# Layer 1 of an S5 and attention encoder: fourteen gate tiles as block quads ahead of k, q and v, branch b inside the S5 stage

## The chip, the cores and the metric

The kernel runs on one core of one Trainium2 chip. The time is the device time of that core in microseconds (us); the time before is the median of three runs. Engines are named as in the profile: PE (TensorE, matrix products), DVE (VectorE), ACT (ScalarE), POOL (GpSimd, here mainly an issuer of DMAs) and SP (SyncE, the issuer of most loads).

## The reference

Two layers, each a token mixer and a feed-forward network, on x of 1024 tokens by 1024 channels, in float32. Of one layer:

```python
hn = rmsnorm(h, norm1_g[layer])
proj = hn @ w_in[layer]          # u 512, q 512, k 128, v 128, gate_a 1024, gate_b 1024
gate_a = sigmoid(proj[..., o_ga:o_gb]); gate_b = sigmoid(proj[..., o_gb:])
y_a = s5_branch(u, ...)          # bidirectional diagonal state space, gelu, GLU
y_b = windowed_gqa(q, k, v, sink, bias, mask)   # 8 heads, window 128
merged = gate_a * (y_a @ w_branch_a[layer]) + gate_b * (y_b @ w_branch_b[layer])
h = h + merged @ w_out[layer]
hn2 = rmsnorm(h, norm2_g[layer])
h = h + (silu(hn2 @ ffn_w_gate[layer]) * (hn2 @ ffn_w_up[layer])) @ ffn_w_down[layer]
```

## The kernel before

Activations lie channels on partitions, in two halves of 512 tokens. A float32 product is three products of fp32r pairs (a high part and a rest): weight high by activation high, weight high by activation low, weight low by activation high. `chain` (L166) does that for each of the K blocks of 128, so a half tile of the input projection (K = 1024, tile `pj`) is 24 matmuls of 128x512, and a half tile of a branch product (K = 512, tile `br`) is 12. `piece` (L179) is the same for one block product of a quad. `fetch` (L116) loads a weight tile with a DMA on SP's queue into one of four buffers `raw`; `parts` (L154) splits it, ACT casting the high part `whi` (L163), DVE subtracting the low part `wlo` (L164).

A quad replaces two tiles over both halves, a 2x2 product of blocks that would take eight block products of 12 matmuls, by seven products of sums of blocks, after Strassen and Winograd. The FFN uses it for gate and up tiles (`quad_items`, L1235): `quad_part` (L130) forms and splits the sums of the weights, `sums` (L1215) those of the activations (`T`, four lists of pairs).

The work is a list of items (`self.seq`) that `build` (L1353) writes in order and `emit` (L193) carries out; weights are split ahead of their use by a few items. Each engine runs its instructions in the order written, with small shifts by the scheduler.

In layer 1, before the change, the order is: the k, v and q tiles, woven with the norm of the second half (`norm_parts`, L1134); the first half tiles of u; `attention_items` (L849), 18 steps. In a step PE does scores `s` of one block, the value product `pv` of an earlier one and the transposes `pt`; DVE does the exponentials' sums and scales (L780, L797). One fill item, a projection half tile of q, u or a gate, is added per step (`per` = 1). From step 12 each step also has one S5 state: `s5_states` (L913), in which PE does 16 small products (`s5x`, L924), DVE the rotation, the scans and the rotation back (L932 to L948), and ACT four copies (`s5sg`, L952). Then `s5_items` (L1007): in each of eight iterations two states, one output (`s5y` on PE, L966 to L969, from the copies of two states), one gelu (DVE L981, ACT tanh L982, DVE L989), the loads of two later states on SP (L899 to L909), and two fill items, the gate tiles that are left. A gate tile (`tile_gate`, L746) ends with a tanh on ACT (L751) and a store to DRAM on POOL's queue (L753). `att_pairs` (L829) splits the attention's output of one group of heads into pairs (ACT L841, DVE L842); in layer 1 both groups come behind the S5 stage, with the GLU (`glu_items`, L1069). Last come the items of branch b and of branch a in turns (`branch_items`, L1046).

Layer 0 has the other order already: its gate tiles are fills of attention and S5, the first pairs stand at step 11 of attention, and its branch-b items fill the S5 stage at 2.2 per iteration together with the gates that are left.

Of the kernel before, what the change touches and what calls it, by code (L numbers as in the profile page):

```python
# [17 lines left out]
P = 128  # L18
# [3 lines left out]
HC = 512  # L22
# [73 lines left out]
class Trunk:  # L96
# [752 lines left out]
    def attention_items(self, l, keys, q23, fill, per, tail):  # L849


        stage = {}
        fill = (list(fill[:2]) if l else []) + q23 + list(fill[2 if l else 0:])

        def scores(u):
            stage[u] = self.att_scores(l, u // 8, u % 8)

        def scale(u):
            self.att_scale(l, u // 8, *stage[u])

# [240 lines left out]
        return early, split, out  # L1101


    def w_out_items(self, l):
        nc, V = self.nc, self.nc.vector
        self.h2 = {}
# [2 lines left out]
        src = self.t["xt"] if l == 0 else self.hs  # L1109
# [43 lines left out]
    def ffn_items(self, l, fill, head):  # L1153

        nc, V = self.nc, self.nc.vector
        ff = [{}, {}]
        quads = QUAD_FROM[l]
        groups = GROUPS[l]
        last = len(groups) - 1
        early = quads < 4  # L1160
        ys = {} if early else None
# [48 lines left out]
        n0, n1 = (self.norm_parts(h, "rf", 2 * l + 1, lambda m, h=h: self.h2[m, h], lambda: self.hn2, ys) for h in range(2))  # L1210
        main = []
        blocks = []
        T = [[None] * 4 for _ in range(4)]

        def sums(j):  # L1215

            at = ((j, 0), (j, 1), (j + 4, 0), (j + 4, 1))
            if early:
                y11, y12, y21, y22 = (ys.pop(a) for a in at)
            else:  # L1220
                y11, y12, y21, y22 = (self.A("y") for _ in at)
                for y, (m, h) in zip((y11, y12, y21, y22), at):
                    hi, lo = self.hn2[h][m]
                    V.tensor_tensor(y, hi.bitcast(F32), lo.bitcast(F32), ADD)
            V.tensor_tensor(y11, y12, y11, SUB)
            V.tensor_tensor(y12, y22, y12, SUB)
            V.tensor_tensor(y22, y22, y11, SUB)
            V.tensor_tensor(y21, y21, y22, SUB)
            for k, y in enumerate((y11, y22, y12, y21)):
                T[k][j] = (y, None)  # L1230

        def sum_pairs(j, k):
            T[k][j] = self.split(T[k][j][0], f"tt{k}")

        def quad_items(f):  # L1235

            q = Quad(self.t["w_gate"][l, f].rearrange("p k c -> p (k c)"), self.t["w_up"][l, f].rearrange("p k c -> p (k c)"))
            b = {}

            def product(bank, g, off, xs, start):  # L1240
                def run():
                    if start:
                        b[bank] = self.PS(f"q{bank}")
                    self.piece(b[bank], g, off, xs(), start)
                return (run, g)

            B = lambda h, a: lambda: self.hn2[h][a:a + 4]
            p = [product("x", q.a, 0, B(0, 0), True), product("y", q.b, HC, lambda: T[1], True),
                 product("v", q.b, 0, lambda: T[0], True), product("x", q.a, HC, B(0, 4), False),
                 product("y", q.c, 0, lambda: T[2], False), product("w", q.d, 0, lambda: T[3], True),  # L1250
                 product("v", q.e, 0, B(1, 4), False)]

            def first():
                b["p1"] = self.A("qp")
# [91 lines left out]
        if fill:  # L1346
            a = len(head) + 12
            b = fill_end
# [4 lines left out]
    def build(self):  # L1353
# [31 lines left out]
        for l in range(DEPTH):  # L1385
# [23 lines left out]
            n0, n1 = (self.norm_parts(h, "ra", 2 * l, lambda m, h=h, src=src: src(m, h), lambda: self.hn) for h in range(2))  # L1409
            v1, v2 = self.halves(vc[0])  # L1410
            loads, states = self.s5_head(l)
            tail_items = {11: pairs[:1] if l == 0 else []}
            for k, (ld, sts) in enumerate(zip(loads, states)):
                a = 18 - 2 * S5_LEAD + k
                tail_items.setdefault(a - 2, []).append(ld)
# [21 lines left out]
            else:  # L1437

                k1, k2 = self.halves(kc[0])
                self.add(tail[:-6] + [n0[0]] + tail[-6:-4] + [n0[1], n0[2], tail[-4], n0[3], tail[-3], n0[4], tail[-2], n0[5],  # L1440
                                                              tail[-1], (start_layer,)] +
                         [k1, n1[0], k2, v1, n1[1], n1[2], v2, n1[3], n1[4], n1[5], qc[0], ke[0], ve[0], qe[0], kc[1], ke[1],
                          vc[1], ve[1]] + keys[:2] + [qc[1], qe[1], vals, bias0] + q1 + us[:2])
# [23 lines left out]
            self.add(early[:3] + split[:3] + left[:n // 2] + early[3:] + (pairs[:1] if l else []) + left[n // 2:n] + split[3:] +  # L1467
                     (self.mix(glu, pairs[1:]) if l else glu))
            left = left[n:]
            if l == 0:  # L1470
                rest = left + ba
            else:
# [141 lines left out]
```

## Time and profile before

| what | us |
|---|---|
| median of three runs | 2656.34 (2655.23 to 2657.16) |
| the profiled execution, its own time | 2654.39 |
| its span on the core | 2652.6 |
| PE busy | 2595.7 |
| DVE busy | 1646.7 |
| ACT busy | 1027.1 |

The span is the stretch from the first to the last instruction; 1.8 us of the execution's time lie around it. The granted clock of PE was 0.993 of full speed on average. A matmul's row lasts 0.39 us from its start to its modelled end, but the next one starts before that: rates are read from starts.

### The profile page before, as it was taken

The numbers are of one execution on the slowest core, as the hardware profiler recorded it, in microseconds if no ns is written. First come the engines' busy times: TensorE is split into PE (matmuls) and PEld (weight loads), VectorE is DVE, ScalarE is ACT, GpSimd is POOL, SyncE is SP. The second block draws the span as 40 slices with busy tenths as digits, with TensorE's granted clock in tenths as the row PEclk, the third lists the DMA queues.
The fourth block names the chain that finished last, engine by engine and source line by source line (L and its number), as shares of the span: only waits on it lengthen the run. The fifth ranks groups of instructions, "written<-read, shape, count | busy, mean of one in ns | idle before, by whom it ended". The sixth has DMA issues, their size and how long they took to land.

```text
span 2652.6 us, 35154 instructions
## 1 busy us (share of the span) xinstructions
PE 2595.7 (98%) x12914; PEld 2112.6 (80%) x12914; DVE 1646.7 (62%) x3481; ACT 1027.1 (39%) x1953; POOL 346.3 (13%) x508
## 2 busy tenths in 40 slices
PE   8999999999999999999999999999999999999997
PEld 6786677887888888888877778888878888888886
DVE  8985878565955655544673576646376545554556
ACT  5335653422333233333344553343235433333332
POOL 0231001000122110121010001100002221122010
PEclk9999999999999999999999999999999999999998
DMA  3453345353255252564342235434315652465253
GB/s 138 144 177 114 125 135 180 123 190 136 70 123 149 89 106 51 120 126 89 78 178 76 72 128 181 149 119 168 127 64 114 132 123 62 91 122 114 60 109 132
DMA packets 153981, 317.16 MB, mean 120 GB/s; under 512 B 20384, under 2 KB 53408, under 8 KB 153808
## 3 DMA queue, kind: packets, MB, share of 16 engines
q1 hardware_dynamic: 105040, 201.68, 23.4%
q0 software_dynamic: 48768, 113.24, 19.5%
q8 instruction: 101, 1.65, 0.2%
q14 instruction: 72, 0.59, 0.1%
HBM read 196.37 MB, written 118.44 MB: 119 GB/s over the span
## 4 chain that ended last, share of the span: by engine, by line
PE 90%; DVE 6%; DMA 2%; ACT 1%; issue 1%; SPq 0%; DVEq 0%; ACTq 0%
PE pj L175 6%; PE pj L176 6%; PE pj L177 6%; PE dn L175 6%; PE dn L176 6%; PE dn L177 6%; PE br L175 2%; PE br L177 2%; PE br L176 2%; PE wo L175 2%; PE wo L176 2%; PE wo L177 2%; PE qy L187 2%; PE qx L187 2%; PE qx L186 2%; PE qy L186 2%
## 5 line engine op out<-in xcount | busy, mean ns | idle before, releaser
L164 DVE TENSOR_TENSOR wlo<-raw,whi 128x1024 fp32r<-128x1024 f32 (+3 forms) x208 | 192.6, 926 | 291.3 <-ACT whi L163 284.4
L163 ACT CAST whi<-raw 128x1024 fp32r<-128x1024 f32 (+3 forms) x208 | 168.6, 811 | 400.3 <-PE pj L176 120.5
L175 PE MATMUL pj<-rah,whi 128*128 128x512 f32 x768 | 306.7, 400 | 0.7 <-ACT rah L112 0.7
L176 PE MATMUL pj<-ral,whi 128*128 128x512 f32 x768 | 301.1, 392 | 1.3 <-DVE ral L113 1.3
L177 PE MATMUL pj<-rah,wlo 128*128 128x512 f32 x768 | 300.2, 391 | 0.0
L1192 POOL DMA_DIRECT2D hs<-dx x192 | 165.3, 862 | 818.7 <-ACT dx L1191 708.3
L175 PEld LDWEIGHTS pj<-rah,whi 128*128 128x128 f32 x768 | 144.9, 189 | 35.0 <-issue 3.1
L176 PEld LDWEIGHTS pj<-ral,whi 128*128 128x128 f32 x768 | 145.2, 189 | 31.2 <-DVE ral L113 3.0
L177 PEld LDWEIGHTS pj<-rah,wlo 128*128 128x128 f32 x768 | 144.9, 189 | 30.9
L1191 ACT COPY dx<-dn 128x512 f32<-128x512 f32 x192 | 111.7, 583 | 86.8 <-PE dn L177 80.9
L780 DVE CUSTOM_DVE_ANT_0 x<-s,bias,nsink 128x384 f32<-128x384 f32 (+1 forms) x128 | 67.8, 580 | 67.4 <-PE s L774 65.8
L952 ACT COPY s5sg<-s5s 64x256 f32<-64x256 f32 x128 | 51.7, 404 | 133.8 <-DVE s5s L947 126.1
L175 PE MATMUL wo<-mgh,whi 128*128 128x512 f32 x256 | 100.0, 391 | 0.0
L177 PE MATMUL wo<-mgh,wlo 128*128 128x512 f32 x256 | 99.7, 389 | 0.0
L176 PE MATMUL wo<-mgl,whi 128*128 128x512 f32 x256 | 99.6, 389 | 0.0
L186 PE MATMUL qx<-rfh,whi 128*128 128x512 f32 x256 | 99.6, 389 | 0.0
L187 PE MATMUL qx<-rfl,whi 128*128 128x512 f32 x256 | 99.6, 389 | 0.0
L188 PE MATMUL qx<-rfh,wlo 128*128 128x512 f32 x256 | 99.6, 389 | 0.0
L112 ACT CAST ffah<-ts 128x512 fp32r<-128x512 f32 x32 | 19.9, 621 | 174.3 <-DVE ts L1274 174.3
L784 ACT ACTIVATE x<-x,sm 128x384 f32<-128x384 f32 (+1 forms) x128 | 73.9, 578 | 21.0 <-DVE sm L780 17.5
L175 PE MATMUL dn<-ffbh,whi 128*128 128x512 f32 x208 | 81.9, 394 | 0.0
L176 PE MATMUL dn<-ffbl,whi 128*128 128x512 f32 x208 | 81.2, 390 | 0.0
(435 smaller groups left out, 6748.6 us busy)
## 6 DMA issues: line engine op xcount, KB each, us to landing
hs<-dx POOLq DMA_DIRECT2D x192, 256.0 KB, 5.7
raw<-in_w_in SPq DMA_DIRECT2D x52, 512.0 KB
raw<-in_w_gate SPq DMA_DIRECT2D x44, 512.0 KB
raw<-in_w_up SPq DMA_DIRECT2D x44, 512.0 KB
g<-th POOLq DMA_DIRECT2D x64, 256.0 KB, 2.8
thr<-g SPq DMA_DIRECT2D x64, 256.0 KB
raw<-in_w_down SPq DMA_DIRECT2D x80, 192.0 KB
hs<-h POOLq DMA_DIRECT2D x48, 256.0 KB, 2.3
```

The costliest lines, as they stand in the source:

```text
L163: nc.scalar.copy(g.hi[:, :n], g.raw[:, :n])
L164: nc.vector.tensor_tensor(g.lo[:, :n], g.raw[:, :n], g.hi[:, :n].bitcast(F32), SUB)
L175: mm(ps, lhsT=wh, rhs=xh, start=k == 0, stop=False)
L176: mm(ps, lhsT=wh, rhs=xl, start=False, stop=False)
L177: mm(ps, lhsT=wl, rhs=xh, start=False, stop=k == n - 1)
L186: mm(ps, lhsT=wh, rhs=xh, start=start and k == 0, stop=False)
L187: mm(ps, lhsT=wh, rhs=xl, start=False, stop=False)
L188: mm(ps, lhsT=wl, rhs=xh, start=False, stop=k == len(xs) - 1)
L780: V.tensor_tensor_reduce(out=x[:, :n], in0=ps[:, :n], in1=self.bias[hd][:, bo:bo + n], op0=ADD, op1=ALU.min, scale=-1.0, scalar=self.nsink ...
L784: nc.scalar.activation(ex[h][:, :n], ex[h][:, :n], AF.Exp, scale=-1.0, bias=nm[:, h:h + 1], accum_out=su[:, h:h + 1])
L1191: nc.scalar.copy(t, ps)
L1192: nc.gpsimd.dma_start(self.hs[m, h], t, accum_op=ADD)
```

## The change

Layer 1 is written in another order, and fourteen of its sixteen gate tiles are computed differently.

- The u tiles come first, woven with the norm of the second half. Beside them DVE and ACT form the block sums of the activations and split them (`sums`, `sum_pairs`, now methods that the FFN shares).
- Seven quads follow, each two gate tiles (all eight of gate b, six of gate a), from `gate_quads`. Each ends in four tanh and four stores.
- Then come k, q and v with their transposes, and attention, with q's last tiles and the two plain gate tiles (8 half-tile items in all) at 0.45 per step. The pairs of head group 0 stand at step 11, those of group 1 behind the steps.
- The fill of the S5 stage is branch b (16 items), 1.35 per iteration.
- The GLU follows, and then branch a alone.

```diff
+GATE_QUADS = 7
...
-        fill = (list(fill[:2]) if l else []) + q23 + list(fill[2 if l else 0:])
+        fill = q23 + list(fill)
...
+    def quad_products(self, src1, src2, pairs, T):
...
+        return [product("x", q.a, 0, B(0, 0), True), product("y", q.b, HC, lambda: T[1], True),
+                product("v", q.b, 0, lambda: T[0], True), product("x", q.a, HC, B(0, 4), False),
+                product("y", q.c, 0, lambda: T[2], False), product("w", q.d, 0, lambda: T[3], True),
+                product("v", q.e, 0, B(1, 4), False)], b
+
+    def gate_quads(self, l, jobs, T):
...
+            def store(n, h, ps, two=two):
+                m0, i, to = two[n]
+                th = self.A(f"th{h}")
+                nc.scalar.activation(th, ps, AF.Tanh, scale=0.5)
+                to[i, h] = self.pd.tile([P, HC], F32, name=f"g{l}_{m0}_{i}_{h}")
+                nc.gpsimd.dma_start(to[i, h], th)
...
-            tail_items = {11: pairs[:1] if l == 0 else []}
+            tail_items = {11: pairs[:1]}
...
-                         [k1, n1[0], k2, v1, n1[1], n1[2], v2, n1[3], n1[4], n1[5], qc[0], ke[0], ve[0], qe[0], kc[1], ke[1],
-                          vc[1], ve[1]] + keys[:2] + [qc[1], qe[1], vals, bias0] + q1 + us[:2])
-                left = self.attention_items(l, keys, q23, us[2:] + gb + ga, 1, tail_items)
+                         [a[0], n1[0], a[1], c[0], n1[1], n1[2], c[1], n1[3], n1[4], n1[5], us[4], *s[:2], us[1], *s[2:], us[3],
+                          *sp[1], us[5], *sp[0], us[6], *sp[2], us[7], *sp[3]] + quads +
+                         [kc[0], kc[1], ke[0], ke[1], bias0, qc[0], *keys[:2], qc[1], qe[0], qe[1], *q1, vc[0], vc[1], ve[0], ve[1],
+                          vals])
+                left = self.attention_items(l, keys, q23, plain, 0.45, tail_items)
+                self.add(pairs[1:])
...
-            if l == 0:
-                left = self.s5_items(l, left + bb, 2.2)
-            else:
-                left = self.s5_items(l, left, 2)
+            left = self.s5_items(l, left + bb, 2.2 if l == 0 else 1.35)
...
-            if l == 0:
-                rest = left + ba
-            else:
-                rest = left + [it for p in zip(bb, ba) for it in p]
-            self.add(rest)
+            self.add(left[n:] + ba)
```

On all of PE the program has 10,637 rows before and 10,553 with the change. Three places show what moved.

PE in the S5 stage of layer 1, before: one `s5x` group between two half tiles (`pj` are projection half tiles of 24 matmuls).

```order
L176 MATMUL pj_15353<-ral,whi 128x512
L177 MATMUL pj_15353<-rah,wlo 128x512
L924 MATMUL s5x<-s5uk,s5wbt 64x128 x8
L175 MATMUL pj_15432<-rah,whi 128x512
L176 MATMUL pj_15432<-ral,whi 128x512
```

PE at the same place with the change (`br` is a branch item of 12 matmuls, `s5y` an output of 12):

```order
L177 MATMUL br<-ybl_15616,whi 128x512
L178 MATMUL br<-ybh_15615,wlo 128x512
L925 MATMUL s5x<-s5uk,s5wbt 64x128 x8
L967 MATMUL s5y<-s5uk 128x128
L969 MATMUL s5y<-s5sg,s5ca 128x127
L970 MATMUL s5y<-s5sg,s5ca 128x127
```

The half tiles are gone from between the groups; one or two branch items of 12 matmuls stand there. Counted over the order, 16 `s5x` groups, the last seven `s5y`, two half tiles and nine branch items lie between the transposes of attention step 11 and the last `s5y`.

DVE behind the last S5 state of the attention steps, with the change (`ybl` are the low parts of the attention's output, written by `att_pairs`):

```order
L948 TENSOR_TENSOR s5s<-s5s,s5c 128x2x128
L949 TENSOR_TENSOR s5s<-s5s,s5c 128x2x128
L843 TENSOR_TENSOR ybl_15604<-yb_14874,ybh_15603 128x4x64
L843 TENSOR_TENSOR ybl_15604<-yb_15310,ybh_15603 128x4x64
L843 TENSOR_TENSOR ybl_15610<-yb_14874,ybh_15609 128x4x64
L843 TENSOR_TENSOR ybl_15610<-yb_15310,ybh_15609 128x4x64
L843 TENSOR_TENSOR ybl_15616<-yb_14875,ybh_15615 128x4x64
L843 TENSOR_TENSOR ybl_15616<-yb_15311,ybh_15615 128x4x64
L843 TENSOR_TENSOR ybl_15622<-yb_14875,ybh_15621 128x4x64
L843 TENSOR_TENSOR ybl_15622<-yb_15311,ybh_15621 128x4x64
L982 SCALAR_TENSOR_TENSOR s5w<-s5g,s5y 128x512
L990 SCALAR_TENSOR_TENSOR s5g<-s5g,s5y 128x512
```

The eight lows of group 1 now stand in the middle of the S5 work, ahead of the first gelu; before, all sixteen came behind the last state. After this place ten states follow, with a gelu after each two.

DVE in the norm of layer 1, with the change (`rs` is the chain of the reciprocal root, `sm<-raw` are sums of the first quad's weights, `sqc` sums of squares):

```order
L89 TENSOR_SCALAR rs<-rsi 128x4
L139 TENSOR_TENSOR sm<-raw 128x512
L294 TENSOR_TENSOR sqc_12249<-sqc_12249,sq 128x512
L89 TENSOR_TENSOR rs<-rs 128x4
L1293 TENSOR_TENSOR h_12236<-h_12236,dn 128x512
L89 SCALAR_TENSOR_TENSOR rs<-rs 128x4
L140 TENSOR_TENSOR sm<-sm,raw 128x512
L89 SCALAR_TENSOR_TENSOR rs<-rs 128x4
```

The two sums of the quad's weights are new in this chain.

## Rows read from the trace of the kernel before

**Rows 1.** The page, busy time: engine, busy us (share of the span), instructions.

```profile
PE 2595.7 (98%) x12914; PEld 2112.6 (80%) x12914; DVE 1646.7 (62%) x3481; ACT 1027.1 (39%) x1953; POOL 346.3 (13%) x508
```

**Rows 2.** Windows, layer 1: PE, PEld, DVE, ACT, POOL busy (instructions), clock, DMA share, GB/s.

```profile
1540.00:1560.00 20.00, 19.79 (x128) 14.91 (x128) 16.14 (x48) 10.04 (x28) 0.54 (x1) 1.00 0.28 94
...
1620.00:1640.00 20.00, 20.00 (x142) 16.86 (x141) 15.37 (x30) 7.58 (x16) 1.61 (x3) 1.00 0.55 186
...
1680.00:1700.00 20.00, 20.00 (x125) 16.72 (x124) 17.08 (x37) 7.16 (x15) 3.60 (x6) 1.00 0.28 90
...
sum 180.00, PE 178.15 PEld 144.69 DVE 124.45 ACT 72.46 POOL 26.52; mean PE 19.79 PEld 16.08 DVE 13.83 ACT 8.05 POOL 2.95
```

**Rows 3.** PE's timeline, layer 1: start, us, engine, line, op, out<-in, count.

```profile
1540.11 1.53 PE L805 MATMUL pt<-cst,x 128*128 128x128 f32 x12
...
1637.94 1.10 PE L924 MATMUL s5x<-s5uk,s5wbt 128*64 128x128 f32 x16
...
1644.63 1.10 PE L924 MATMUL s5x<-s5uk,s5wbt 128*64 128x128 f32 x16
...
1654.02 1.10 PE L924 MATMUL s5x<-s5uk,s5wbt 128*64 128x128 f32 x16
...
1707.63 0.39 PE L175 MATMUL pj<-rah,whi 128*128 128x512 f32 x1
...
1713.07 0.38 PE L966 MATMUL s5y<-s5uk 128*128 128x128 f32 x2
```

**Rows 4.** Groups of PE, 1540 to 1716: count | busy, mean ns | idle before.

```profile
L175 PE MATMUL pj<-rah,whi 128*128 128x512 f32 x169 | 67.8, 401 | 0.0
...
L805 PE MATMUL pt<-cst,x 128*128 128x128 f32 x56 | 7.7, 280 | 1.6 <-ACT th L751 1.1 <-DVE sm L780 0.5
```

**Rows 5.** Windows, the quads of layer 0's FFN.

```profile
1200.00:1220.00 20.00, 20.00 (x89) 16.53 (x89) 13.12 (x20) 6.31 (x11) 0.00 (x0) 1.00 0.10 30
```

**Rows 6.** DVE's timeline in layer 0's S5 stage.

```profile
432.12 0.68 DVE L932 TENSOR_TENSOR s5a<-s5x,s5tb 128x512 f32<-128x512 f32 x1
...
439.67 0.69 DVE L989 SCALAR_TENSOR_TENSOR s5g<-s5g,s5y 128x512 f32<-128x512 f32 x1 [1.47 <-ACT s5g L982]
...
440.27 0.68 DVE L932 TENSOR_TENSOR s5a<-s5x,s5tb 128x512 f32<-128x512 f32 x1
...
445.67 0.68 DVE L932 TENSOR_TENSOR s5a<-s5x,s5tb 128x512 f32<-128x512 f32 x1
...
448.21 1.23 DVE L164 TENSOR_TENSOR wlo<-raw,whi 128x1024 fp32r<-128x1024 f32 x1 [1.26 <-ACT whi L163]
```

**Rows 7.** Timelines of DVE and PE in layer 0's attention tail.

```profile
303.95 1.41 DVE L797 TENSOR_SCALAR x<-x,sm 128x384 f32<-128x384 f32 x4
...
305.47 4.71 DVE L842 TENSOR_TENSOR ybl<-yb,ybh 128x256 fp32r<-128x256 f32 x8
...
310.00 1.65 PE L805 MATMUL pt<-cst,x 128*128 128x128 f32 x12
...
351.58 1.14 DVE L797 TENSOR_SCALAR x<-x,sm 128x256 f32<-128x256 f32 x4
```

**Rows 8.** The page's groups: ACT's state copies.

```profile
L952 ACT COPY s5sg<-s5s 64x256 f32<-64x256 f32 x128 | 51.7, 404 | 133.8 <-DVE s5s L947 126.1
```

**Rows 9.** Groups of DVE, 1540 to 1720.

```profile
L164 DVE TENSOR_TENSOR wlo<-raw,whi 128x1024 fp32r<-128x1024 f32 x11 | 13.5, 1224 | 24.3 <-ACT whi L163 23.4 <-PE s5y L966 0.9
```

**Rows 10.** PE's timeline in layer 0's S5 stage.

```profile
456.15 1.97 PE L924 MATMUL s5x<-s5uk,s5wbt 128*64 128x128 f32 x16 [5.54 <-DMA s5uk<-ud]
```

**Rows 11.** Windows, layer 0's S5 stage.

```profile
450.00:460.00 10.00, 4.46 (x24) 3.35 (x23) 8.40 (x20) 3.21 (x7) 2.37 (x4) 0.66 0.55 177
```

**Rows 12.** PE's timeline, norm of layer 1.

```profile
1351.37 2.07 PE L325 MATMUL psn<-cst,rs 128*128 128x128 f32 x8 [2.52 <-DVE rs L88]
```

**Rows 13.** SP's queue in layer 0's S5 stage.

```profile
449.46 0.34 SPq L124 DMA_DIRECT2D raw<-in_w_br_a  x1
...
451.28 0.43 SPq L904 DMA_DIRECT2D s5uk<-ud  x1
```

More of the change, by code (lines that the diff above doesn't have):

```diff
@@ L1101, in glu_items, with sums @@
         return early, split, out
+    def sums(self, T, ys, pairs, j):
+        V = self.nc.vector
+        at = ((j, 0), (j, 1), (j + 4, 0), (j + 4, 1))
+        if ys is not None:
+            y11, y12, y21, y22 = (ys.pop(a) for a in at)
+        else:
+            y11, y12, y21, y22 = (self.A("y") for _ in at)
+            for y, (m, h) in zip((y11, y12, y21, y22), at):
+                hi, lo = pairs[h][m]
+                V.tensor_tensor(y, hi.bitcast(F32), lo.bitcast(F32), ADD)
+        V.tensor_tensor(y11, y12, y11, SUB)
+        V.tensor_tensor(y12, y22, y12, SUB)
+        V.tensor_tensor(y22, y22, y11, SUB)
+        V.tensor_tensor(y21, y21, y22, SUB)
+        for k, y in enumerate((y11, y22, y12, y21)):
+            T[k][j] = (y, None)
@@ new lines, in sum_pairs, with product, run @@
+    def sum_pairs(self, T, j, k):
+        T[k][j] = self.split(T[k][j][0], f"tt{k}")
+    def quad_products(self, src1, src2, pairs, T):
+        q = Quad(*(s.rearrange("p k c -> p (k c)") for s in (src1, src2)))
+        b = {}
+        def product(bank, g, off, xs, start):
+            def run():
+                if start:
+                    b[bank] = self.PS(f"q{bank}")
+                self.piece(b[bank], g, off, xs(), start)
+            return (run, g)
+        B = lambda h, a: lambda: pairs()[h][a:a + 4]
+        return [product("x", q.a, 0, B(0, 0), True), product("y", q.b, HC, lambda: T[1], True),
+                product("v", q.b, 0, lambda: T[0], True), product("x", q.a, HC, B(0, 4), False),
+                product("y", q.c, 0, lambda: T[2], False), product("w", q.d, 0, lambda: T[3], True),
+                product("v", q.e, 0, B(1, 4), False)], b
@@ new lines, in gate_quads, with first, second, out11 @@
+    def gate_quads(self, l, jobs, T):
+        nc, V = self.nc, self.nc.vector
+        out, nxt = [], []
+        for two in jobs:
+            p, b = self.quad_products(*(self.t["w_in"][l, m0 + i] for m0, i, _ in two), lambda: self.hn, T)
+            def store(n, h, ps, two=two):
[4 more added lines that the diff above has]
+                nc.gpsimd.dma_start(to[i, h], th)
+            def first(b=b):
+                b["p1"] = self.A("qp")
+                nc.scalar.copy(b["p1"], b["x"])
+            def second(b=b):
+                b["u2"] = self.A("qu")
+                V.tensor_tensor(b["u2"], b["p1"], b["y"], ADD)
+            def out11(b=b, store=store):
+                store(0, 0, b["x"])
+            def out22(b=b, store=store):
+                V.tensor_tensor(b["p1"], b["p1"], b["y"], ADD)
+                c = self.A("qc")
+                V.tensor_tensor(c, b["p1"], b["v"], ADD)
+                store(1, 1, c)
+            def out21(b=b, store=store):
+                V.tensor_tensor(b["p1"], b["p1"], b["w"], ADD)
+                store(1, 0, b["p1"])
+            def out12(b=b, store=store):
+                V.tensor_tensor(b["u2"], b["u2"], b["v"], ADD)
+                store(0, 1, b["u2"])
+            nxt.append((p, [(fn,) for fn in (first, second, out11, out22, out21, out12)]))
+        for k, (p, e) in enumerate(nxt):
+            if k == 0:
+                out.append(p[0])
+            out += [p[1], e[0], p[2], e[1], p[3], p[4], e[2], p[5], e[3]]
+            if k + 1 < len(nxt):
+                out.append(nxt[k + 1][0][0])
+            out += [e[4], p[6], e[5]]
+        return out
@@ L1215, in sums @@
         def sums(j):
-            at = ((j, 0), (j, 1), (j + 4, 0), (j + 4, 1))
-            if early:
-                y11, y12, y21, y22 = (ys.pop(a) for a in at)
-            else:
[L1221 to L1230, printed above, removed]
+            self.sums(T, ys, self.hn2, j)
         def sum_pairs(j, k):
-            T[k][j] = self.split(T[k][j][0], f"tt{k}")
+            self.sum_pairs(T, j, k)
         def quad_items(f):
[L1237 to L1251, printed above, removed]
+            p, b = self.quad_products(self.t["w_gate"][l, f], self.t["w_up"][l, f], lambda: self.hn2, T)
             def first():
@@ L1439, in build @@
                 k1, k2 = self.halves(kc[0])
+                both = [(M_GB, i, tb) for i in range(8)] + [(M_GA, i, ta) for i in range(8)]
+                n = 2 * GATE_QUADS
+                quads = self.gate_quads(l, [both[i:i + 2] for i in range(0, n, 2)], T)
+                plain = (gb + ga)[2 * n:]
+                s = [(lambda j=j, T=T, ys=ys: self.sums(T, ys, self.hn, j),) for j in range(4)]
+                sp = [[(lambda j=j, k=k, T=T: self.sum_pairs(T, j, k),) for j in range(4)] for k in range(4)]
+                a, c = (self.halves(x) for x in (us[0], us[2]))
                 self.add(tail[:-6] + [n0[0]] + tail[-6:-4] + [n0[1], n0[2], tail[-4], n0[3], tail[-3], n0[4], tail[-2], n0[5],
                                                               tail[-1], (start_layer,)] +
-                         [k1, n1[0], k2, v1, n1[1], n1[2], v2, n1[3], n1[4], n1[5], qc[0], ke[0], ve[0], qe[0], kc[1], ke[1],
-                          vc[1], ve[1]] + keys[:2] + [qc[1], qe[1], vals, bias0] + q1 + us[:2])
-                left = self.attention_items(l, keys, q23, us[2:] + gb + ga, 1, tail_items)
+                         [a[0], n1[0], a[1], c[0], n1[1], n1[2], c[1], n1[3], n1[4], n1[5], us[4], *s[:2], us[1], *s[2:], us[3],
[4 more added lines that the diff above has]
+                self.add(pairs[1:])
             def done_b(m, h, ps):
@@ L1461, in build @@
             early, split, glu = self.glu_items(l)
[L1462 to L1465 removed]
+            left = self.s5_items(l, left + bb, 2.2 if l == 0 else 1.35)
             n = min(4, len(left))
[L1467 to L1474 removed]
+            self.add(early[:3] + split[:3] + left[:n // 2] + early[3:] + left[n // 2:n] + split[3:] + glu)
+            self.add(left[n:] + ba)
             ffn = self.ffn_items(l, self.s5_prep_items(1) if l == 0 else None, self.w_out_items(l))
```

4 lines of the change are left out of this document (3 added, 1 removed).

## The prediction

> **What bounds the kernel now.** I read the page's busy shares first, then the windows of layer 1, then timelines inside its attention and S5 stages. TensorE (PE) is busy in 98% of the span, 2595.7 of 2652.6 us, so it leaves 57 us idle in all; VectorE (DVE) is at 62% [rows 1]. The windows show what the average hides: in layer 1's attention tail and S5 stage DVE is busy for 15 to 17 us of every 20 while PE loses almost nothing [rows 2]. Over 1540 to 1720 us DVE works 124.45 us and PE 178.15 of 180. PE is the bound there only because projection work lies between the short S5 products: 169 first passes of `pj`, which is 21 half tiles, and 1.6 us of waits [rows 4]. This change takes just that work away from the stage, so its worth is read there.
>
> **Prices on PE.** From 1707.63 to 1713.07 lie the 24 matmuls of one half tile: 5.44 us, 0.2267 us each [rows 3]. A branch item is 12 of them, 2.72 us. The S5 products start at 1637.94, 1644.63 and 1654.02 [rows 3]; the first gap is one half tile and one `s5x` group, so `s5x` costs 6.69 - 5.44 = 1.25 us; the second holds `s5y` too, 9.39 - 6.69 = 2.70 us.
>
> **Step 1, fourteen gate tiles as seven quads.** A quad is seven block products of 12 matmuls, 84, where two tiles took 96. Seven quads save 84 matmuls, 84 x 0.2267 = **-19.0 us** of PE work. What they add on DVE and ACT (block sums, casts, lows) I cost at nothing: the quads of the FFN do the same per quad, and there PE is full at 20.00 of 20 with DVE at 13.12 and ACT at 6.31 [rows 5]. The sums of the activations (16 subtractions, 16 lows on DVE) lie beside eight `u` half tiles, 43.5 us of PE. The 56 stores of gates move with the quads on POOL's queue, 13% busy [rows 1], ahead of the loads that read them back only in branch a. If a cover failed, the stalls would add to the forecast, which leaves 15 us above it in the range.
>
> **Step 2, the gates leave the attention tail and the S5 stage.** The stretch from the transposes of attention step 11 (1540.11) to the last `s5y` (1713.07) now takes 173.0 us [rows 3]: 21 half tiles, 21 x 5.44 = 114.2; about 1.85 idle (180 less 178.15 [rows 2]); the rest, 57.0, is attention and S5 work that stays. In the changed order only two half tiles and nine branch-b items remain in the same stretch (the other seven follow the last `s5y`). PE's work there becomes 57.0 + 2 x 5.44 + 9 x 2.72 = **92.4 us**.
>
> DVE's chain over the stretch does not shrink with it. One S5 state takes 440.27 to 445.67 = 5.40 us from start to start, and two states with one gelu take 432.12 to 445.67 = 13.55 us; in it the gelu pair waits 1.47 us for ACT's tanh [rows 6]. A weight low costs 1.23 us. From the scale of step 11 to that of step 15, one state per step, layer 0 took 303.95 to 351.58 = 47.6 us, pairs of head group 0 (4.71 us) in it [rows 7]. Layer 0 did table work of the next states there as well, about 1 us a step by my estimate; I take 44.6. Then, as the changed order has them on DVE: the scale, three states, a low and the output copies, 1.4 + 16.2 + 1.2 + 0.6 = 19.4; the pairs of group 1 behind ACT's four state copies (4 x 0.404 [rows 8]) and a first cast (0.6 by estimate, like DVE's low of the same tile), and the first gelu, 1.6 + 0.6 + 4.7 + 2.7 = 9.6; states 6 to 15 with four gelus between, 5 x 13.55 - 2.75 = 65.0; two more lows 2.4; the last state copies 1.6. Sum **142.6 us** until the last `s5y` may start. PE's stretch begins 6 us after that scale (303.95 to 310.00 [rows 7]). So PE is idle for 142.6 - 6.0 - 92.4 = **44 us, where it was idle for 1.85**: +42 us.
>
> The bound from below: only DVE's busy time counts, and its waits get filled. Of its 124.45 us the 11 weight lows of the stretch, 13.5 us [rows 9], go, and four lows (4.9) and both pairs (9.4) come: 125.2, so idle is at least 125.2 - 6.0 - 92.4 = 27 us. From above: the 47.6 us untrimmed and one low more, 48 us. I take 44, since the cadence of 13.55 us is from the same loop with branch items as its fill.
>
> Behind the late `s5y` wait the seven last branch items, 19 us of PE, and they cover the chain through the last gelu to the GLU; so no second stall is priced there.
>
> **Step 3, clock.** After an idle of 5.54 us in layer 0 the next `s5x` took 1.97 instead of 1.10 us [rows 3], and the window 450 to 460 has a mean granted clock of 0.66 [rows 10, 11]: part of it at 1.2 GHz instead of 2.4. A slow spell inside the stage falls into time in which PE would wait anyway; only the one after the last wait lengthens the path, 4 us of work at half speed, **+2 us** (0 to +5).
>
> **Step 4, the order at the front.** With `u` first, two DVE sums of the first quad's weights stand inside the norm's rstd chain, where PE already waits 2.52 us for DVE [rows 12]: two adds of the kind that takes 0.69 us (the second row of the gelu pair [rows 6]) give **+1.2 us** (0 to +3). The transposes of v now follow its last half tile at once, with ACT's copies to wait for: **+1.3 us** by estimate, two ACT operations of 0.6 (0 to +3). Layer 0 keeps its order, 0.
>
> **The sum** against the profiled execution of 2654.39 us: 2654.4 - 19.0 + 42 + 2 + 1.2 + 1.3 = 2681.9. Its DVE chain is assembled from steps that may overlap a little at their joints, so I place it 3 us lower, 2679; the median of the runs stands 2 us above that execution: **2681 us**. A measurement of this kernel can tell about 0.2%, 5.3 us, from no change.
>
> The Trainium skill (Perfetto Trace Analysis, Optimization Strategy) says that where the most-contended engine changes from stage to stage, interleaving the stages may improve the time. This change goes the other way: it takes PE's heavy work out of DVE's heavy stage; the rows agree that the interleaved stage left PE 1.6 us of waits.
>
> **Rivals.**
> *A, the saving stays (faster).* PE remains the bound in the stage, so that only the 84 matmuls count: 2656.3 - 19.0 + 2.5 = 2640. For it speaks PE's 98%. It decides if DVE's two states and a gelu take no more than PE's 2 x 1.25 + 2.70 + 1.35 x 2.72 = 8.9 us; the row says 13.55, and even 10.8 of pure states exceeds it. Chance 0.05. The Trainium skill (Perfetto Trace Analysis, Identifying the Most-Contended Engine) says to optimise the engine of highest occupancy first; on the whole span that is PE, and by that rule alone the time would be this 2640.
> *B, DVE's waits are filled.* The lower bound, 27 us idle: -19 + 25 + 2 + 2.5, that is 2656 + 10.5 = 2667 us; without the clock and the front 2662. Chance 0.27, among it 0.05 that it ends within 0.2%.
> *C, S5 loads come late as well.* In layer 0 the raw weight fetch of branch a was issued at 449.46, after the low of 448.21, the S5 loads stood behind it on the same SP queue, and PE waited 5.54 us for `s5uk` [rows 6, 10, 13]. In the changed layer 1 the branch-b fetches share that queue with the S5 loads. Once or twice: +6 to +14, 2687 to 2695. Chance 0.18.
> *D, the change does not shorten PE's work.* The order lists 10,553 PE rows instead of 10,637, exactly 84 fewer; so none.
> The forecast itself, 2672 to 2687: 0.50.
>
> The range 2661 to 2696 takes in B to C and leaves A out, with tails. Faster by over 0.2%: 0.05; within 0.2%: 0.05; slower: 0.90.
>
> **What would show it.** PE's matmul count falls by 84. The quad stretch has PE at 20.00 of 20. In the windows of layer 1's attention tail and S5 stage PE falls to 12 to 16 of 20, DVE rises to 17 or more; pairs of `s5x` come every 13 to 14 us instead of 16.1; the waits name `s5y` behind ACT's state copies and DVE. PE's busy sum falls by about 17 to 19, its idle rises by 40 or more. I am wrong if PE stays over 19 of 20 there (A), if idle in the stage is under 30 us (B), or if a wait of several us on an S5 load appears (C).

## The result and the profile after

The changed kernel takes 2684.63 us, median of four runs (2683.24 to 2688.17), against 2656.64 us of the kernel before (four runs of each): a ratio of 1.0112, 95% interval 1.01 to 1.0124, 28 us slower. The forecast was 2681 with 2661 to 2696. The profiled execution after took 2688.17 us (span 2686.4), the longest of the four; the profiles differ by 33.8 us of span, of which the medians have 28.

The busy shares on the page of the changed kernel, against [rows 1]:

```profile
PE 2597.3 (97%) x12830; PEld 2110.7 (79%) x12830; DVE 1714.7 (64%) x3597; ACT 1053.0 (39%) x1997; POOL 345.5 (13%) x508
```

There are 84 matmul rows fewer, 12830 for 12914, yet PE is busy 1.6 us longer, because part of the matmuls ran at half clock. DVE's busy time rose by 68 us: 54.5 of them go with the quads (the run with plain gate tiles below has 1660.2), 13.5 with the rest, the sums of the activations among it. PE's idle time is 2686.4 - 2597.3 = 89.1 us, before 56.9.

The windows of layer 1's attention tail and S5 stage after, against [rows 2] (PE, PEld, DVE, ACT, POOL busy with instructions, granted clock, DMA share, GB/s):

```profile
1720.00:1740.00 20.00, 13.39 (x93) 10.71 (x89) 15.92 (x37) 9.24 (x20) 0.54 (x1) 0.82 0.81 259
...
1740.00:1760.00 20.00, 19.26 (x130) 15.40 (x131) 17.50 (x37) 9.37 (x20) 3.83 (x7) 0.84 0.19 59
...
1760.00:1780.00 20.00, 12.87 (x108) 11.32 (x106) 17.02 (x37) 6.64 (x14) 3.35 (x6) 0.83 0.65 206
...
1800.00:1820.00 20.00, 14.18 (x57) 12.05 (x56) 15.57 (x31) 8.93 (x18) 4.75 (x8) 0.66 0.18 53
```

PE, which lost 1.85 of 180 us in this stage before, falls to 12.87 of 20, with a granted clock of 0.66 to 0.84 in these four windows; DVE works 15.6 to 17.5 of 20 in them. Above, the quads' stretch is full:

```profile
1440.00:1460.00 20.00, 20.00 (x90) 16.57 (x89) 10.69 (x16) 7.24 (x11) 2.17 (x4) 1.00 0.29 106
```

DVE's timeline of the changed kernel, at the scale of attention step 11, that of step 15, and the first operation of the S5 states 6, 8 and 15, answers to [rows 6, 7] (a row that runs past the end of the window asked for shows only a part of its count and duration; its start and its wait are whole):

```profile
1669.33 0.42 DVE L798 TENSOR_SCALAR x<-x,sm 128x384 f32<-128x384 f32 x1
...
1714.88 0.62 DVE L798 TENSOR_SCALAR x<-x,sm 128x256 f32<-128x256 f32 x2
...
1744.59 0.69 DVE L933 TENSOR_TENSOR s5a<-s5x,s5tb 128x512 f32<-128x512 f32 x1
...
1758.13 0.68 DVE L933 TENSOR_TENSOR s5a<-s5x,s5tb 128x512 f32<-128x512 f32 x1
...
1806.52 0.68 DVE L933 TENSOR_TENSOR s5a<-s5x,s5tb 128x512 f32<-128x512 f32 x1
```

From step 11 to step 15 it takes 45.6 us, from there to state 6 29.7, from state 6 to state 15 61.9. Two states and a gelu take 1744.59 to 1758.13 = 13.54 us, as in layer 0 [rows 6]. PE's timeline over the same stretch, from the transposes of step 11 to the last `s5y`, against [rows 3]:

```profile
1676.34 0.55 PE L806 MATMUL pt<-cst,x 128*128 128x128 f32 x3
...
1687.96 0.59 PE L925 MATMUL s5x<-s5uk,s5wbt 128*64 128x128 f32 x6 [3.80 <-issue]
...
1723.97 0.69 PE L821 MATMUL pv<-p,vt 128*64 128x256 f32 x2 [3.39 <-ACT p L808]
...
1773.67 0.70 PE L925 MATMUL s5x<-s5uk,s5wbt 128*64 128x128 f32 x4 [7.13 <-DMA s5uk<-ud]
...
1814.01 0.58 PE L969 MATMUL s5y<-s5sg,s5ca 128*128 128x127 f32 x1 [3.62 <-ACT s5sg L953]
```

The last wait ends at 1814.01, 144.7 us after the scale of step 11. PE's stretch is 137.7 us long, for work that the prediction put at 92.4 us at full clock. The idle times inside it add up to 30.9 us. The other 14 are what is left, and I put them down to half clock; the window over the stretch, 106.69 us busy at a mean granted clock of 0.88, gives some 13 by itself:

```profile
1676.34:1814.01 137.67, 106.69 (x733) 83.46 (x731) 117.80 (x287) 61.01 (x146) 13.55 (x23) 0.88 0.43 135
```

Of PE's waits in the whole execution two groups have most of their time here:

```profile
PE s5x L925 <- DMA s5uk<-ud: 12.6, 2, 7.1
...
PE s5y L969 <- ACT s5sg L953: 8.4, 3, 3.6
```

The first has 7.13 us in layer 1 and the rest in layer 0; the second was not on the list of the kernel before. DVE's own waits between the scale of step 11 and 1814.01 (two of those on ACT and the only one on PE):

```profile
DVE s5g L990 <- ACT s5g L983: 6.6, 5, 1.5
DVE sm L795 <- ACT sm L788: 5.9, 4, 2.1
...
DVE yb L828 <- PE pv L821: 1.8, 1, 1.8
```

DVE is busy for 124.3 of the 144.7 us and waits for 18.2, nearly all of it for ACT: for the gelu's tanh, for the sums of the exponentials, for casts. So what is called DVE's chain below is work of DVE and ACT in turns. In the attention steps ACT takes the exponentials behind its copies of the S5 state before, and for these it waits for DVE (three waits from 1680 to 1716, 16.8 us together); then DVE waits for the exponentials' sums. DVE never waits for an `s5x` there; in the same stage of the kernel before it did, for PE had no time left:

```profile
DVE s5a L932 <- PE s5x L924: 8.7, 7, 1.6
```

### The profile page after: what moved, and what is told of

Read it like the earlier page. It is cut to its first block, busy times and chain, and to the rows that moved or that the text cites. A ratio compares the mean times of both kernels' runs of the same rounds, so it can differ in the third digit from the quotient of the medians.

```text
span 2686.4 us, 35141 instructions
## 1 busy us (share of the span) xinstructions
PE 2597.3 (97%) x12830; PEld 2110.7 (79%) x12830; DVE 1714.7 (64%) x3597; ACT 1053.0 (39%) x1997; POOL 345.5 (13%) x508
## 4 chain that ended last, share of the span: by engine, by line
PE 86%; DVE 8%; ACT 3%; DMA 2%; issue 1%; SPq 0%; POOL 0%; DVEq 0%; ACTq 0%; POOLq 0%
PE dn L176 6%; PE dn L177 6%; PE dn L178 6%; PE pj L176 4%; PE pj L177 4%; PE pj L178 4%; PE qy L188 3%; PE qx L188 3%; PE qy L187 3%; PE qx L187 3%; PE qx L189 3%; PE qy L189 3%; PE qv L188 3%; PE qv L187 3%; PE qv L189 3%; PE wo L177 2%
## 5 line engine op out<-in xcount | busy, mean ns | idle before, releaser
L165 DVE TENSOR_TENSOR wlo<-raw,whi 128x1024 fp32r<-128x1024 f32 (+3 forms) x194 | 175.3, 904 | 263.1 <-ACT whi L164 263.0
L164 ACT CAST whi<-raw 128x1024 fp32r<-128x1024 f32 (+3 forms) x194 | 154.1, 795 | 343.9 <-issue 75.5
L176 PE MATMUL pj<-rah,whi 128*128 128x512 f32 x544 | 218.5, 403 | 2.3 <-DVE sm L781 1.3
L177 PE MATMUL pj<-ral,whi 128*128 128x512 f32 x544 | 215.1, 396 | 1.3 <-DVE ral L114 1.3
L178 PE MATMUL pj<-rah,wlo 128*128 128x512 f32 x544 | 214.1, 394 | 0.0
L176 PEld LDWEIGHTS pj<-rah,whi 128*128 128x128 f32 x544 | 103.6, 190 | 26.8 <-DVE sm L781 2.1
L177 PEld LDWEIGHTS pj<-ral,whi 128*128 128x128 f32 x544 | 104.0, 191 | 23.6 <-DVE ral L114 3.2
L178 PEld LDWEIGHTS pj<-rah,wlo 128*128 128x128 f32 x544 | 103.7, 191 | 22.1
L785 ACT ACTIVATE x<-x,sm 128x384 f32<-128x384 f32 (+1 forms) x128 | 73.8, 578 | 18.7 <-DVE sm L781 15.0
```

Source lines behind the costliest of these rows:

```text
L164: nc.scalar.copy(g.hi[:, :n], g.raw[:, :n])
L165: nc.vector.tensor_tensor(g.lo[:, :n], g.raw[:, :n], g.hi[:, :n].bitcast(F32), SUB)
L176: mm(ps, lhsT=wh, rhs=xh, start=k == 0, stop=False)
L177: mm(ps, lhsT=wh, rhs=xl, start=False, stop=False)
L178: mm(ps, lhsT=wl, rhs=xh, start=False, stop=k == n - 1)
L785: nc.scalar.activation(ex[h][:, :n], ex[h][:, :n], AF.Exp, scale=-1.0, bias=nm[:, h:h + 1], accum_out=su[:, h:h + 1])
```

## The experiments

The theory, called D: DVE's chain of attention scales, states and gelus sets the length of this stage once the half tiles have left, and the quads save what their matmuls cost. Its rivals were half clock (P), late loads (L) and costs of the quads (Q). The experiments are compared with the 2684.63 us of the changed kernel, which was not timed again beside them; the kernel before was, and its median lay between 2654.59 and 2656.64, so a difference of 2 us or less between two of these kernels says nothing.

### The quads alone undone

```diff
-                quads = self.gate_quads(l, [both[i:i + 2] for i in range(0, n, 2)], T)
+                quads = (gb + ga)[:2 * n]
```

> The changed kernel with the fourteen gate tiles as plain tiles in the quads' place; nothing else moves (the sums of the activations are still formed, unused). Theory D (VectorE's chain sets the length of the attention tail and S5 stage, and the quads give their full saving in a stretch that TensorE fills): the 84 matmuls come back at 0.2267 us, 2684.6 + 19.0 = 2703.6 us (2700 to 2707). Rival Q (the quads lose part of their saving to block sums and splits, and that is a part of the loss): 2690 to 2698.

2703.29 us, 18.7 us above the changed kernel. Its page has the 84 matmuls again:

```profile
PE 2610.2 (97%) x12914; PEld 2122.4 (79%) x12914; DVE 1660.2 (61%) x3513; ACT 1036.7 (38%) x1969; POOL 346.7 (13%) x508
```

So the quads give their whole saving, and Q falls. Without them the new order alone costs 2703.3 - 2656.2 = 47 us.

### A shorter state, after and before

```diff
-        V.tensor_tensor(Sv[:, :, 0], Sv[:, :, 0], bv[:, :, 0], SUB)
-        V.tensor_tensor(Sv[:, :, 1], Sv[:, :, 1], bv[:, :, 1], ADD)
+        if l == 0:
+            V.tensor_tensor(Sv[:, :, 0], Sv[:, :, 0], bv[:, :, 0], SUB)
+            V.tensor_tensor(Sv[:, :, 1], Sv[:, :, 1], bv[:, :, 1], ADD)
```

> The changed kernel, with the last two additions of each S5 state of layer 1 left out on VectorE, so that layer 1's S5 branch isn't the reference's. A state is shorter by 0.68 us, 16 states 10.9 us; TensorE has the same work. Theory D: 2684.6 - 10.9 = 2673.7 us (2671 to 2677). Rival P (TensorE at half clock sets the stage): 2683 to 2686, no gain. Rival L (late loads of the S5 operands set it): less than half the gain, 2679 to 2685.

2668.84 us, 15.8 us less and 2 us below the range. DVE's timeline of this kernel: the scale of step 11 and the first operations of the states 14 and 15.

```profile
1667.84 0.42 DVE L798 TENSOR_SCALAR x<-x,sm 128x384 f32<-128x384 f32 x1
...
1788.12 0.68 DVE L933 TENSOR_TENSOR s5a<-s5x,s5tb 128x512 f32<-128x512 f32 x1
...
1792.73 0.68 DVE L933 TENSOR_TENSOR s5a<-s5x,s5tb 128x512 f32<-128x512 f32 x1
```

A state takes 4.61 us instead of 5.40, which is 0.79 less and not 0.68: the first of the two additions had also started 0.11 us later behind the product that it needs (0.71 us, 1748.60 to 1749.31 in the changed kernel) than the operation that now follows that product (0.60 us). The chain to state 15 takes 124.9 instead of 137.2 us, so 12.3 of the gain lie there. PE's work is unchanged. With P there would have been no gain, with L less than half of the forecast one. But with the shorter chain one load does reach DVE, at state 5, where PE had waited 4.04 us for `s5uk`:

```profile
1727.02 0.69 DVE L933 TENSOR_TENSOR s5a<-s5x,s5tb 128x512 f32<-128x512 f32 x1 [4.21 <-PE s5x L925]
```

So L does not set the changed kernel's time, but its loads have only a few us to spare.

> The kernel before, with the same two additions of each S5 state of layer 1 left out on VectorE, so that layer 1's S5 branch isn't the reference's. VectorE has 12 us less to do there, as in the changed kernel, where that gave 15.8 us. Theory D: before, TensorE set this stage, so nothing or next to nothing, 2654 to 2657 us. If VectorE's chain set the stage before as well: 2641 to 2646.

The same edit in the kernel before: 2653.00 us against 2655.57, a ratio of 0.9991 (0.9982 to 1.0001), 1 us below the range. A window of its S5 stage:

```profile
1640.00:1660.00 20.00, 20.00 (x134) 16.41 (x132) 13.82 (x28) 8.71 (x18) 3.59 (x6) 1.00 0.74 242
```

PE is full in all nine windows from 1540 to 1720, and the time that DVE saves is idle. The same edit is worth 15.8 us in one order and 2.6 us, not clear of no change, in the other: the bound has gone from PE to DVE's chain.

### The S5 loads on another queue

```diff
         st = {}
+        queue = nc.sync if l == 0 else nc.gpsimd
...
-            nc.sync.dma_start(st[nm], self.sp[l][q][k])
+            queue.dma_start(st[nm], self.sp[l][q][k])
```

> The changed kernel with the S5 loads of layer 1 issued on POOL's queue instead of SP's, so that they no longer stand behind a weight fetch that waits for its buffer. Rival L: the wait of 7.13 us on the operand's load goes and the time with it, 2677 to 2679 us. Theory D: the wait goes from the list, VectorE had two states' inputs in hand while TensorE waited, and the time stays, 2682 to 2687.

2682.81 us (2679.18 to 2687.87), a ratio of 1.0112 to the kernel before (1.009 to 1.0134), the same as the changed kernel's. Both L and D had expected the wait to go. It did not; it was split over more loads. PE's waits, and DVE's timeline from the scale of step 11 to state 15:

```profile
PE s5x L926 <- DMA s5uk<-ud: 19.5, 6, 6.0
```

```profile
1665.34 0.42 DVE L798 TENSOR_SCALAR x<-x,sm 128x384 f32<-128x384 f32 x1
...
1801.95 0.68 DVE L934 TENSOR_TENSOR s5a<-s5x,s5tb 128x512 f32<-128x512 f32 x1
```

PE waits longer in all for such loads, and DVE's chain takes 136.6 us, as it took 137.2. DVE's state at 1774.04 in the changed kernel began without a wait although PE had just waited 7.13 us for a load, because its own input had been there before that wait. In the kernel of this run, too, DVE has no wait for an `s5x` in the stage. What was not tried is a way that ends these waits; that they cost nothing is shown in so far as DVE's chain is as long with 7.1 us of them in the stage as with 13.5.

### Branch b out of the stage

```diff
-            left = self.s5_items(l, left + bb, 2.2 if l == 0 else 1.35)
+            if l == 0:
+                left = self.s5_items(l, left + bb, 2.2)
+            else:
+                left = self.s5_items(l, left, 1.35) + bb
```

> The changed kernel with all sixteen branch-b items behind the S5 stage, which has no fill then. Theory D: the nine items that lay in TensorE's idle time, 9 x 2.72 = 24.5 us, stand in the open, while VectorE's chain is shorter by the weight lows only (3 us): 2706 us (2702 to 2710). If the branch-b items and their loads were what slowed the stage: 2685 to 2695.

2704.18 us, 19.6 us above the changed kernel. A window of its S5 stage, the wait that grew, and DVE's rows from the scale of step 11 to state 15:

```profile
1740.00:1760.00 20.00, 10.88 (x66) 10.00 (x67) 18.23 (x42) 5.95 (x14) 3.49 (x6) 0.59 0.72 224
```

```profile
PE s5y L969 <- ACT s5sg L953: 32.2, 10, 9.6
```

```profile
1663.04 0.42 DVE L798 TENSOR_SCALAR x<-x,sm 128x384 f32<-128x384 f32 x1
...
1797.73 0.69 DVE L933 TENSOR_TENSOR s5a<-s5x,s5tb 128x512 f32<-128x512 f32 x1
```

PE is idle for nearly half the time and has a mean clock of 0.59 when it works; from 1740 to 1800 us it is busy for 33.00 of 60. DVE's chain still takes 134.7 us (137.2 with the items in the stage and two of their weight lows between). Of the items' 24.5 us 19.6 appear in the open, so in the stage they had cost 5 us at most, and half clock on PE does not lengthen the stage while PE has time left.

### Fewer quads, and half tiles as fill

```diff
-GATE_QUADS = 7
+GATE_QUADS = 5
...
-            want = min(len(fill), round(per * (i + 1)) + max(0, i - 15))
+            want = min(len(fill), round(per * (i + 1)) + max(0, i - 15) + (round(0.5 * max(0, i - 11)) if l else 0))
...
+            if l:
+                m, left = left, []
+                while m:
+                    left += m[:1] + bb[:2]
+                    m, bb = m[1:], bb[2:]
-            left = self.s5_items(l, left + bb, 2.2 if l == 0 else 1.35)
+            left = self.s5_items(l, left + bb, 2.2 if l == 0 else 2)
```

> The changed kernel with five quads instead of seven; of the eight half tiles that this leaves, three to four go into the attention tail and the rest into the S5 stage between the branch-b items (2 per iteration). Work of TensorE 2 x 12 matmuls = 5.4 us more in all, in the stage that the chain bounds some 44 us more. Theory D: the new work lies in TensorE's idle time, 2684.6 + 5.4 - 39 = 2651 us (2646 to 2658), four weight lows of 1.2 us on VectorE counted. If TensorE's waits there can't be filled (they end too late for another order): 2675 to 2690.

2663.51 us: 21 us better than the changed kernel, though it has 5.4 us more of PE work, but 12 us above the expectation and outside both ranges. DVE's timeline behind the scale of step 15:

```profile
1678.32 0.61 DVE L798 TENSOR_SCALAR x<-x,sm 128x256 f32<-128x256 f32 x2
...
1689.96 0.49 DVE L828 COPY yb<-pv 128x128 f32<-128x128 f32 x2 [2.81 <-PE pv L821]
...
1692.01 0.69 DVE L933 TENSOR_TENSOR s5a<-s5x,s5tb 128x512 f32<-128x512 f32 x1 [1.56 <-PE s5x L925]
...
1700.58 1.23 DVE L165 TENSOR_TENSOR wlo<-raw,whi 128x1024 fp32r<-128x1024 f32 x1 [3.08 <-ACT whi L164]
...
1721.29 0.68 DVE L933 TENSOR_TENSOR s5a<-s5x,s5tb 128x512 f32<-128x512 f32 x1
```

Four half tiles, 21.8 us of PE, stand ahead of the last products of attention and of states 4 and 5, and DVE waits for PE there. From the scale to state 6 it takes 43.0 us instead of 29.7. The waits for PE are only 5.2 us of these 13.3 (7.1 in four waits, for 1.8 in the changed kernel). Two weight lows more are 2.5, and waits for ACT's casts of the weights, of which the changed kernel has none here, are 5.0. So a half tile as fill has a price on DVE as well, which the expectation counted as the lows alone.

The next kernel, with five quads too, lays the half tiles one per step and then among the branch-b items, with the tiles of v ahead of k:

```diff
+            if l:
+                want = round(per * (min(i, 12) + 1)) + max(0, i - 12)
...
-                left = self.attention_items(l, keys, q23, plain, 0.45, tail_items)
+                left = self.attention_items(l, keys, q23, plain, 0.55, tail_items)
...
+            left = self.s5_items(l, left + bb, 2.2 if l == 0 else 1.85)
```

> Five quads, as in the run before, but the left half tiles laid where VectorE's chain leaves TensorE time: one per attention step from step 13 on, four in the S5 stage between pairs of branch-b items, and the tiles of v ahead of k, so that its transposes need not wait. In the run before, four half tiles at the end of attention kept VectorE waiting (from the scale of step 15 to state 6 it took 43.0 instead of 29.7 us). Theory D: TensorE's idle time in the stage falls to about 10 us: 2656.4 - 13.6 + 10 + 4 (front) = 2656 us (2651 to 2660). If the place of the half tiles doesn't matter: 2662 to 2665 again.

2666.73 us (ratio 1.0045, 1.003 to 1.006): no better than the run before and above both ranges, a miss. Waits that its PE timeline shows:

```profile
1559.77 0.69 PE L806 MATMUL pt<-cst,x 128*128 128x128 f32 x2 [2.82 <-DVE x L798]
...
1737.54 0.55 PE L928 MATMUL s5x<-s5uk,s5wbt 128*64 128x128 f32 x6 [2.49 <-DMA s5uk<-ud]
...
1750.87 0.70 PE L928 MATMUL s5x<-s5uk,s5wbt 128*64 128x128 f32 x4 [5.59 <-ACT s5sg L956]
```

They have moved: to the start of attention, where v's transposes no longer wait but the first scale does, and to state loads and state copies in the S5 stage.

> The same with four quads: TensorE's work is 10.9 us less than before, and some eleven half tiles and nine branch-b items fill the stage, 57 + 60 + 24.5 = 141 us of TensorE's work against a chain of 138 + 6 on VectorE. Theory D: hardly any idle time is left, 2656.4 - 10.9 + 4 (front) + 4 = 2653 us (2649 to 2657), the best of the versions with quads. If VectorE's chain gets longer by each half tile as in the run with five quads: 2660 to 2668.

This is the same edit with `GATE_QUADS = 4`, 0.7 and 2.15 for the rates, and the branch-b items one by one between the half tiles. 2658.84 us, a ratio of 1.0011 (1.0002 to 1.002), 2 us above the range. In its PE timeline two waits of over 2 us are left in layer 1 behind the norm:

```profile
1547.44 0.69 PE L806 MATMUL pt<-cst,x 128*128 128x128 f32 x2 [2.82 <-DVE x L798]
...
1775.84 0.70 PE L928 MATMUL s5x<-s5uk,s5wbt 128*64 128x128 f32 x4 [2.44 <-DMA s5uk<-ud]
```

### The front

```diff
-                         [a[0], n1[0], a[1], c[0], n1[1], n1[2], c[1], n1[3], n1[4], n1[5], us[4], *s[:2], us[1], *s[2:], us[3],
-                          *sp[1], us[5], *sp[0], us[6], *sp[2], us[7], *sp[3]] + quads +
+                         [k1, n1[0], k2, v1, n1[1], n1[2], v2, n1[3], n1[4], n1[5], us[0], ke[0], ve[0], kc[1], *s[:2], ke[1], vc[1],
+                          ve[1], us[1], *s[2:], us[2], us[3], *sp[1], us[4], us[5], *sp[0], us[6], *sp[2], us[7], *sp[3]] + quads +
```

> The changed kernel, seven quads, with the front of layer 1 as before: k and v woven with the norm's second half, then u, the sums and the quads; the transposes of v stand behind q's first tile, and the sums of the first quad's weights are out of the norm's chain. Attention, the S5 stage and branch b as in the changed kernel. Theory D with the front counted by hand from the two traces (3.9 us at the norm, 1.4 at the transposes of v): 2684.6 - 5 = 2679.5 us (2677 to 2682). If the order of the front costs nothing, and half clock falls there by chance: 2683 to 2686.

2684.26 us, a ratio of 1.0113 (1.0097 to 1.0128): no gain. Its profile does have the second rstd product sooner than the changed kernel's (1377.84, below):

```profile
1374.36 0.49 PE L326 MATMUL psn<-cst,rs 128*128 128x128 f32 x3
```

That gain is of one execution. With the front of the changed kernel, its own profile reaches the scale of step 11 at 1669.33, and those of two kernels that differ from it only later at 1665.34 and 1663.04; this kernel does at 1665.31. So the 4 us that I had read off two traces lie within what one execution differs from the next, and the order of the front is not shown to cost anything.

> Four quads with the half tiles spread over the stage as in the run before, the front of layer 1 as in the kernel before, and a second fill item ahead of attention's first transposes (where 2.8 us were lost). Theory D: 2658.8 - 4 - 2.8 = 2652 us (2649 to 2655), under the 2655.6 of the kernel before. If the waits only move: 2657 to 2660.

Four quads, that front, and `math.ceil` in place of `round` in the rate: 2655.03 us against 2654.59, a ratio of 1.0001 (0.9992 to 1.001). That is 3 us above the expectation and just outside its range. The three least full windows of its stage:

```profile
1660.00:1680.00 20.00, 18.50 (x124) 13.99 (x121) 16.83 (x53) 11.65 (x33) 1.08 (x2) 1.00 0.50 159
...
1720.00:1740.00 20.00, 18.18 (x120) 14.88 (x119) 16.53 (x35) 9.58 (x20) 4.73 (x8) 0.92 0.57 182
...
1760.00:1780.00 20.00, 17.65 (x134) 15.18 (x135) 18.22 (x42) 7.92 (x18) 4.55 (x8) 1.00 0.54 170
```

PE is nearly full again, 17.65 to 18.50 of 20 at the least, and the kernel is level with the one before, not under it. PE's 10.9 us of saving are gone again, by the waits that are left, as far as these windows show. No version tried beats the kernel before.

## Why the prediction was right, step by step

That DVE works 15 to 17 of every 20 us in the old stage, as the prediction reads [rows 2], holds for six of its nine windows; from 1580 to 1620 it is 12.67 and 8.29, at the end 5.22. No term of the sum uses it.

**Step 1**, the quads, -19.0: shown, 18.7 by the run with plain gates, and PE is full in their stretch.

**Step 2**, the stage, +42: shown. DVE's chain was put at 142.6 us and took 144.7: to step 15 45.6 for 44.6, to state 6 29.7 for 29.0, then 69.4 to the last wait (61.9 to state 15 and that state with a low and its copies) for 69.0. PE's stretch was to be idle for 44 us; 45.3 us of it were not full-speed work. I said idle and found idle for two thirds: 30.9 us idle and 14 us of half clock, which takes the place of idling as step 3 says. For the same reason two signs that I had named did not come: PE's busy sum rose by 1.6 us instead of falling by 17 to 19, and its idle time rose by 32.2 and not by 40 or more. PE's transposes began 7.0 us behind the scale, not 6.0. The 44.6 us to step 15 rested on an estimate of layer 0's table work that no row or run shows; that part measured 45.6. The lower bound, with DVE's waits filled, did not come true: DVE's busy time was 124.3 us, for 125.2 in that bound, and its waits stayed; the pair of states keeps its 13.54 us, and 15.91 where a weight low stands in it (1758.13 to 1774.04).

**Step 3**, clock, +2: the trace shows it, though no run takes it by itself. Behind the last wait the matmuls start 0.43 us apart until 1818.02 and 0.23 us apart from then on:

```profile
1817.59 0.60 PE L176 MATMUL br<-ybh,whi 128*128 128x512 f32 x1
...
1818.27 0.40 PE L178 MATMUL br<-ybh,wlo 128*128 128x512 f32 x1
1818.50 0.40 PE L176 MATMUL br<-ybh,whi 128*128 128x512 f32 x1
```

The last rows of `s5y` take 2.15 us up to the first of `br`, where the same rows at full speed took 1.14 (1799.46 to 1800.60), and four matmuls of `br` 1.86 for 0.91: 4.0 us at half speed, which cost 2.0.

**Step 4**, the front, +1.2 and +1.3: this is the step that fell. I put the two sums of the quad's weights into the rstd chain; the wait there got shorter, 1.64 us instead of the 2.52 of [rows 12]. Over all profiles it looks otherwise: with the changed front this wait is 1.57 to 3.53 us in eight of them (1.64 in five), with the front of before 0.85, 0.85, 0.92 and the 2.52. So the sums may well cost some 0.8 us there, which one pair of profiles hides. What took longer in the profile was the norm's second half:

```profile
1353.95 0.49 PE L326 MATMUL psn<-cst,rs 128*128 128x128 f32 x2 [1.64 <-DVE rs L89]
...
1377.84 0.49 PE L326 MATMUL psn<-cst,rs 128*128 128x128 f32 x3
...
1592.52 0.55 PE L720 MATMUL vt<-cst,kv 128*128 128x128 f32 x3 [1.44 <-ACT kv L696]
```

The same product in the kernel before:

```profile
1373.09 0.49 PE L325 MATMUL psn<-cst,rs 128*128 128x128 f32 x3
```

It comes 4.75 us later; 1.2 of these were there when the norm's first wait began (1343.35 against 1342.18). The windows over it, first of the changed kernel, then of the kernel before:

```profile
1372.00:1378.00 6.00, 6.00 (x18) 4.90 (x19) 1.96 (x12) 0.00 (x0) 0.56 (x1) 0.52 0.11 44
```

```profile
1372.00:1378.00 6.00, 6.00 (x32) 5.09 (x31) 3.77 (x9) 2.15 (x4) 0.00 (x0) 1.00 0.00 0
```

The granted clock is 0.52 there, half the work, behind waits of 1.03 and 0.79 us for the norm's first tiles; the kernel before had waits of 0.66 and 0.79 and kept 1.00. The longer wait alone does not explain it: the runs with shorter states, with the loads on POOL's queue and with branch b behind had the longer waits too (1.03 or 1.04, and 0.8) and kept 1.00 in their window from 1360. What decides it stays open. The run with the front of before removed the spell in its profile and gained nothing in its median. The wait at v's transposes, 1.44 us, is the one that I priced at 1.3. With the front of before it is gone, and from the second rstd product to the scale of step 11 its profile takes 290.95 us (1374.36 to 1665.31) instead of 291.49, so some half a microsecond of it is in the time.

Over the two profiles: -19.0, +43.4 in the stage (45.3 less the 1.85 of before), 4.8 up to the end of the norm, 1.4 at v's transposes, 1.3 in three short waits at the start of attention that I had not priced (0.52, 0.55 and 0.26), together 31.9 of the 33.8 us. The rest, 1.9, is the half-speed spell of step 3. These 33.8 us are of the longest of the four executions, and the 4.8 at the norm lie within the spread of executions. The 28 us of the medians are nearly the stage alone: -19.0 + 43.4 + 2.0 and half a microsecond at v are 27.

In part the forecast's closeness is luck. The 3 us that I took off for overlaps at the joints were not there, since the chain was 2.1 us longer than its sum; the 2.5 us of the front, mostly not shown, stood against them.

**The rivals.** A (the saving stays) is excluded: the shorter state gains 15.8 us. B (waits filled) is excluded by the cadence, though the idle time of 30.9 us is close to the 30 that I had set as its sign. C happened in form and not in time: its sign of my being wrong came, PE did wait 7.13 us for an S5 load, but DVE's chain went on. That the load was late because a branch fetch stood ahead of it on SP's queue is not shown either, since on POOL's queue the waits stayed. I had priced that wait as if PE's idle were the path.

The rule of the Trainium skill on stages with different busiest engines (Perfetto Trace Analysis, Optimization Strategy) was borne out both ways: the new order, which takes the half tiles out of DVE's stage, cost 47 us with plain gate tiles, and laying part of them in again, with fewer quads, brought back 18 to 30. The rule of the Trainium skill to optimise the engine of highest occupancy first (Perfetto Trace Analysis, Identifying the Most-Contended Engine), read on the whole span, would have given the faster rival; PE has the highest share there, by its weight loads too (80% [rows 1]), by which that section judges TensorE. The measurement decides against that reading here.

## What to carry to other kernels

Work that fills a stage bound by another engine can be nearly free there and cost most of its length elsewhere (here at most 5 of 24.5 us against 19.6), as long as it brings that engine little work and is not laid so thickly that it comes late, as with five quads. So before taking fill out, compare the chain of the other engine with what stays on the full one, from rows of that stage and not from the shares of the span. A cadence that one layer shows with the same kind of fill (13.55 us in layer 0) carried over to the other here, 13.54 us, where no weight low stood in it.

## What the runs showed that was not expected

PE ran at a mean clock of 0.59 through 60 us (branch b behind the stage), and the stage was no longer for it. So a low granted clock in a window is no sign by itself of lost time.

The same work on PE and DVE, in the same order, reached the scale of step 11 at 1663.04 to 1669.33 us in four profiles, a spread of 6.3 us and more than the 4 us that I tried to read off two of them. All of it is there at the second rstd product of the norm (1371.51 to 1377.84); from it to that scale the four take 291.48 to 291.53 us. The half-clock spell of the norm (0.83 over 20 us) lay in the window from 1340 in three profiles of changed kernels, in the one from 1360 in five, and in two in neither: a few us of front can't be judged from single profiles.
